# Turning rows over for cross attention: from TensorE transposes to grouped loads and 32x32 blocks on VectorE

## The chip, the cores and the metric

The kernel runs on one core of a Trainium2 chip. The metric is the device time of one execution in microseconds (us). The core has a matrix engine (TensorE, PE in the rows, with its weight loads as PEld), a vector engine (VectorE, DVE), a scalar engine (ScalarE, ACT), GpSimd (POOL) and SyncE (SP), whose queue issues most of the DMA transfers. Each engine takes its own instructions in the order in which they were listed when the program was built, and waits on semaphores where it needs another engine's result.

## The reference, cut to what matters

One encoder layer: a token mixer, then cross attention of 1024 rows into 256 memory tokens, then a mixture of experts. All is f32. The change concerns the cross attention alone:

```
def memory_cross_attention(h, hm, w_q, w_kv, w_o):
    q = (h @ w_q).reshape(Bq, S, N_XATTN_HEADS, XATTN_HEAD_DIM)
    kv = (hm @ w_kv).reshape(Bq, M, 2, N_XATTN_HEADS, XATTN_HEAD_DIM)
    k, v = kv[:, :, 0], kv[:, :, 1]
    s = jnp.einsum('bshd,bmhd->bhsm', q, k).astype(jnp.float32) * (XATTN_HEAD_DIM ** -0.5)
    p = jax.nn.softmax(s, axis=-1).astype(h.dtype)
    o = jnp.einsum('bhsm,bmhd->bshd', p, v).reshape(Bq, S, N_XATTN_HEADS * XATTN_HEAD_DIM)
    return o @ w_o
...
x = x + memory_cross_attention(rms_norm(x, g_xattn[l]), rms_norm(mem, g_mem[l]),
                               w_q_x[l], w_kv_x[l], w_o_x[l])
```

## The kernel before

The 1024 rows are eight tiles of 128, taken in the order of `corder`. The query weights and the keys are multiplied together ahead (the matrix `aH` + `aL`, 1024 x 1024), and so are values and output weights (`vH` + `vL`). So a tile x (128 x 1024) needs two products: its **scores**, x times `a` (4 heads x 256 memory tokens, so 1024 columns), and after the softmax its **values**, p times `v`, 1024 columns that are added to x.

A matmul contracts over the partitions, so both products need their left operand turned over: 1024 columns as eight blocks of 128 partitions. `transposed` (L732) does that: eight PE transposes against the identity (L738) into two PSUM tiles of 128 x 512, `tp`. Every f32 operand is then cut in two by `split` (L107): the high part is a cast on ACT (L108, `xH<-tp`), the low part a subtraction on DVE (L109, `xL<-tp,xH`). `mm3` makes three matmuls of one product: high times high (L100), high `x` in the low matrix (L101), low `x` in the high matrix (L102; only this one reads `xL`).

The loop over the tiles of the scores has two halves of 512 columns (two heads each), 24 matmuls each. Behind the first half's matmuls it calls `prep` for the next tile (L746): load the row tile from `x1_dram`, transpose and split it, sum its squares. Then each half's softmax on DVE and ACT: row maximum (L862), its scaling (L863), two exponentials (ACT, L866), reciprocal (L868), two scalings (L871). The probabilities go to `p_dram` (L872). Of the first tile `prep` is called before the loop, ahead of the last `proj` (the mixer's output product, `pc` in the rows), into the PSUM tile `pa`.

The loop over the tiles of the values has two halves of 24 matmuls as well. Behind the first half's it calls `attend_T` for the next tile (L835): load the probabilities again, transpose and split them. The result is added to x on DVE (L1111), its squares are summed on ACT (L1120), GpSimd makes the reciprocal root (L1122, L1123), and DVE writes the normed row `hn` (L1128). Between them DVE does the routing of the tiles before to the experts, in many small operations.

Which instruction comes when on each engine is not written out here: a scheduler lists the instructions of each engine when the program is built. SP's queue carries the loads of the tiles, the stores of the probabilities and the loads of expert weights (`wraw`), in one order.

Of the kernel before, what the change touches and what calls it, by code (L numbers as in the profile page):

```python
# [9 lines left out]
F32 = mybir.dt.float32  # L10
F32R = mybir.dt.float32r
BF16 = mybir.dt.bfloat16
I32 = mybir.dt.int32
AF = mybir.ActivationFunctionType
ALU = mybir.AluOpType
# [3 lines left out]
P = 128  # L19
D = 1024  # L20
S = 1024
KT = D // P
NT = S // P
NH = 4
DH = 128
NMEM = 256
# [22 lines left out]
def tile_hybrid_encoder(ctx: ExitStack, tc: tile.TileContext,  # L49
                        x, mem, pcols, rows, w_tm, w_cm, w_sT, w_out,  # L50
                        w_kv, w_qT, w_o, w_r, g_moe, g_final, w_gu, w_dn, out, dbg=None):
    nc = tc.nc

    def tpool(**kw):
        return tc.tile_pool(reuse_waits="tile", **kw)
# [33 lines left out]
    p_dram = tc.dram_tile([NT, P, NH * NMEM], F32, name="p_dram")  # L89
# [3 lines left out]
    x1_dram = tc.dram_tile([NT, P, D], F32, name="x1_dram")  # L93

    def rstd_of(dst, ss, n, eps, width=1):
        nc.gpsimd.tensor_scalar(dst, ss, 1.0 / n, eps, op0=ALU.mult, op1=ALU.add)  # L96
        nc.gpsimd.tensor_tensor(dst, dst, mhalf[:, 0:width], op=ALU.pow)  # L97

    def mm3(o, ah, al, bh, bl, first, last):
        nc.tensor.matmul(o, ah, bh, start=first, stop=False)  # L100
        nc.tensor.matmul(o, ah, bl, start=False, stop=False)  # L101
        nc.tensor.matmul(o, al, bh, start=False, stop=last)  # L102

    def f32(t):
        return t.bitcast(F32)

    def split(h, l, r):  # L107
        nc.scalar.copy(h, r)  # L108
        nc.vector.tensor_tensor(l, r, f32(h), op=ALU.subtract)  # L109
# [138 lines left out]
    with ExitStack() as pa:  # L248
# [24 lines left out]
        with tc.manual_schedule(engines={mybir.EngineType.DVE, mybir.EngineType.Activation}):  # L273
# [3 lines left out]
            for kp in range(4):  # L277
                tp = ptr.tile([P, 2, NMEM], F32, name="tp")
# [105 lines left out]
    with tpool(name="work1b", bufs=2, side="right") as work, \  # L384
# [6 lines left out]
        for g in range(4):  # L391
            cm_unit(g + 2)
            for hf in range(2):
                ps = cm_half(g, hf)
                sp = ptr.tile([P, 4, P], F32, name="tp")
                for j in range(4):
# [12 lines left out]
                                               op0=ALU.add, op1=ALU.mult)  # L409
# [5 lines left out]
    with tpool(name="work2", bufs=2, side="right") as work:  # L415
# [9 lines left out]
        for c in range(12):  # L425
# [16 lines left out]
            if c < 8:  # L442
                for hf in range(2):
# [3 lines left out]
                                            op0=ALU.mult, op1=ALU.add)  # L447
                    for w in range(1, 5):
                        nc.vector.scalar_tensor_tensor(cv, pre[:, a + w:a + w + 512], cw[:, c, w:w + 1], cv,
                                                       op0=ALU.mult, op1=ALU.add)  # L450
# [23 lines left out]
    work = pS2.enter_context(tpool(name="work3", bufs=2, side="right"))  # L474
# [252 lines left out]
    pp = pM.enter_context(tpool(name="pp", bufs=2, side="right"))  # L727
    pA = ExitStack()
    apool = pA.enter_context(tpool(name="apool", bufs=1, side="right"))
# [3 lines left out]
    def transposed(src, tile, hl=None):  # L733
        hl = hl or (pp.tile([P, KT, P], F32R, name="xH"), pp.tile([P, KT, P], F32R, name="xL"))
        for g in range(2):
            tp = tile()
            for j in range(4):
                nc.tensor.transpose(tp[:, j], src[:, (g * 4 + j) * P:(g * 4 + j + 1) * P], ident)  # L738
            gs = slice(g * 4, g * 4 + 4)
            split(hl[0][:, gs], hl[1][:, gs], tp)  # L740
        return hl

    def sums(junk, xt, ss):
        nc.scalar.activation(junk, xt, AF.Square, accum_out=ss)

    def prep(c, tile):  # L746
        xt = pp.tile([P, D], F32, name="x1t")
        nc.sync.dma_start(xt, x1_dram[c])
        ss = pp.tile([P, 2], F32, name="ss")
        hl = transposed(xt, tile)  # L750
        sums(xt, xt, ss[:, 0:1])
        rstd_of(ss[:, 0:1], ss[:, 0:1], D, RMS_EPS)
        nc.gpsimd.tensor_scalar(ss[:, 1:2], ss[:, 0:1], -1.0, None, op0=ALU.mult)
        return ss, hl

    for kt in range(KT):
# [3 lines left out]
        aL.append(pair[:, sl])  # L760
        evac(aH[kt], aL[kt], araw[kt // 2][:, sl], gx[:, kt:kt + 1])
    nxt = prep(corder[0], lambda: psa.tile([P, NH, P], F32, name="pa"))
    proj(corder[-1])
    pY.close()
# [18 lines left out]
    work = pV.enter_context(tpool(name="work5", bufs=2))  # L783
# [50 lines left out]

    def attend_T(c):  # L835
        prf = work.tile([P, NH * NMEM], F32, name="pr")
        nc.sync.dma_start(prf, p_dram[c])
        return transposed(prf, trt)

    def attend_x(c):  # L840
        xt = pp.tile([P, D], F32, name="x1t")
        nc.sync.dma_start(xt, x1_dram[c])
        return xt

    for t, c in enumerate(corder):
        ss, (xH, xL) = nxt
        pr = work.tile([P, NH, NMEM], F32, name="pr")
        mx = rw.tile([P, NH], F32, name="smx")
        sm = rw.tile([P, NH], F32, name="ssm")
        for hf in range(2):  # L850
            ps = pmm.tile([P, 512], F32, name="mm")
            sl = slice(hf * 512, hf * 512 + 512)
            for kt in range(KT):
                mm3(ps, xH[:, kt], xL[:, kt], aH[kt][:, sl], aL[kt][:, sl], kt == 0, kt == KT - 1)
            if hf == 0:
                if t + 1 < NT:
                    nxt = prep(corder[t + 1], trt)
                else:
                    nxt = attend_T(corder[0])
            psv = ps.rearrange("p (h m) -> p h m", h=2)  # L860
            hs = slice(hf * 2, hf * 2 + 2)
            nc.vector.tensor_reduce(mx[:, hs], psv, axis=AX.X, op=ALU.max)  # L862
            nc.vector.tensor_scalar(mx[:, hs], mx[:, hs], ss[:, 1:2], None, op0=ALU.mult)  # L863
            for i in range(2):
                h = hf * 2 + i
                nc.scalar.activation(pr[:, h], psv[:, i], AF.Exp, bias=mx[:, h:h + 1], scale=ss[:, 0:1],  # L866
                                     accum_out=sm[:, h:h + 1])
            nc.vector.reciprocal(sm[:, hs], sm[:, hs])  # L868
            for i in range(2):
                h = hf * 2 + i  # L870
                nc.vector.tensor_scalar(pr[:, h], pr[:, h], sm[:, h:h + 1], None, op0=ALU.mult)  # L871
        nc.sync.dma_start(p_dram[c], pr.rearrange("p h m -> p (h m)"))  # L872
        r = work.tile([P, D], F32, name="hn")
        nc.sync.dma_start(r, vw_dram[t])
        split(vH[t], vL[t], r)
# [37 lines left out]
    src = {b: (w_gu[b], w_dn[b]) for b in range(FIXED)}  # L913
# [167 lines left out]
    xt = attend_x(corder[0])  # L1081
    prep_r(2)
    prev = None
    for t, c in enumerate(corder):
# [9 lines left out]
        for hf in range(2):  # L1094
            ps = pmm.tile([P, 512], F32, name="mm")
            sl = slice(hf * 512, hf * 512 + 512)
            for i in range(8):
                mm3(ps, pH[:, i], pL[:, i], vH[i][:, sl], vL[i][:, sl], i == 0, i == 7)
                if t and hf == 0 and i == 1:
                    route_x(prev, 1)  # L1100
                if t > 1 and hf == 0 and i == 2:
                    route_s(t - 2, corder[t - 2])
                if t and hf == 0 and i == 4:
                    route_l(prev)
                if hf and i == 4:
                    route_x(c, 0)
            if t and hf:
                route_w(prev)
                route_p(t - 1, prev)
                route_r(prev)  # L1110
            nc.vector.tensor_tensor(xt[:, sl], xt[:, sl], ps, op=ALU.add)  # L1111
            if hf == 0:
                hn = work.tile([P, D], F32, name="hn")
                if not last:
                    nxt = attend_T(nx)
                else:
                    xgs.append(pp.tile([P, D], F32, name="x1t"))
                    nc.gpsimd.memset(xgs[0], 0.0)
                prep_r(min(3 + 2 * t, NRA))
            nc.scalar.activation(hn[:, sl], xt[:, sl], AF.Square, scale=D ** -0.5, accum_out=ssq[:, hf:hf + 1])  # L1120
# [12 lines left out]
        else:  # L1133
            prev = c
            xt = xn
# [449 lines left out]
```

## Time and profile before

| | |
|---|---|
| median of 3 runs | 1384.59 us (1383.39 to 1385.33) |
| the profiled execution | 1385.45 us, span 1383.7 us |
| mean granted clock of TensorE | 0.971 |
| busy: PE, DVE, ACT, POOL | 1271.4, 793.1, 612.9, 188.3 us |

The span is the time from the first to the last instruction; the profiled execution's own time has 1.75 us around it. Busy times are sums over all stages, so the stage of the change has to be read by itself. In the rows, a matmul's start shows when PE took it up; matmuls overlap, so the steps from start to start tell what one costs, not the durations. "[idle before <-releaser]" is the time for which the engine stood still before the instruction and what ended it. The granted clock (PEclk) is a share of full speed: 1.00 is 2.4 GHz and 0.50 is 1.2 GHz.

### The profile page before, as it was taken

The numbers are of one execution on the slowest core, as the hardware profiler recorded it, in microseconds if no ns is written. First come the engines' busy times: TensorE is split into PE (matmuls) and PEld (weight loads), VectorE is DVE, ScalarE is ACT, GpSimd is POOL, SyncE is SP. The second block draws the span as 40 slices with busy tenths as digits, with TensorE's granted clock in tenths as the row PEclk, the third lists the DMA queues.
The fourth block names the chain that finished last, engine by engine and source line by source line (L and its number), as shares of the span: only waits on it lengthen the run. The fifth ranks groups of instructions, "written<-read, shape, count | busy, mean of one in ns | idle before, by whom it ended". The sixth has DMA issues, their size and how long they took to land. (4 is left out here: it accounts for less than half of the span.)

```text
span 1383.7 us, 18356 instructions
## 1 busy us (share of the span) xinstructions
PE 1271.4 (92%) x6505; PEld 970.5 (70%) x6505; DVE 793.1 (57%) x1532; ACT 612.9 (44%) x1043; POOL 188.3 (14%) x283
## 2 busy tenths in 40 slices
PE   6899999999897899999999679999999999999980
PEld 6899888888886788888888557655555555566530
DVE  5643465883477765753467668645546454667512
ACT  7632343331474442653222248545446454556522
POOL 2000100000021111110133221112111111100012
PEclk9999999999999999999999879999999999999995
DMA  8820122311798652543963568999999999999967
GB/s 317 267 74 1 36 80 84 92 38 42 236 310 283 215 187 100 199 141 108 338 248 112 213 223 313 388 399 402 399 393 395 392 377 391 378 386 379 384 230 265
DMA packets 86750, 339.53 MB, mean 245 GB/s; under 512 B 12008, under 2 KB 24488, under 8 KB 62081
## 3 DMA queue, kind: packets, MB, share of 16 engines
q1 hardware_dynamic: 72672, 304.53, 59.0%
q0 software_dynamic: 11536, 26.31, 6.6%
q10 hardware_dynamic: 2448, 7.51, 1.4%
q8 instruction: 52, 0.85, 0.3%
q14 instruction: 42, 0.34, 0.1%
HBM read 297.06 MB, written 50.67 MB: 251 GB/s over the span
## 5 line engine op out<-in xcount | busy, mean ns | idle before, releaser
L109 DVE TENSOR_TENSOR wl<-wraw,wh 128x1024 fp32r<-128x1024 f32 (+2 forms) x276 | 325.2, 1210 | 118.2 <-ACT wh L108 106.5
L108 ACT CAST wh<-wraw 128x1024 fp32r<-128x1024 f32 (+2 forms) x276 | 277.7, 1037 | 97.4 <-PE mm L101 29.8
L1191 PE MATMUL gu<-wraw,xTn 128*64 128x512 f32 x512 | 118.2, 598 | 0.5 <-DMA wraw<-in_w_gu_dram 0.5
L101 PE MATMUL gu<-wl,xH 128*128 128x512 f32 x272 | 109.4, 402 | 1.3 <-DVE wl L109 1.1
L102 PE MATMUL gu<-wh,xL 128*128 128x512 f32 x272 | 107.6, 396 | 0.0
L100 PE MATMUL gu<-wh,xH 128*128 128x512 f32 x272 | 99.3, 405 | 2.4 <-ACT wh L108 1.7
L100 PE MATMUL mm<-hH,wh 128*128 128x512 f32 x256 | 100.3, 392 | 0.8 <-ACT wh L108 0.8
L101 PE MATMUL mm<-hL,wh 128*128 128x512 f32 x256 | 100.2, 391 | 0.0
L102 PE MATMUL mm<-hH,wl 128*128 128x512 f32 x256 | 100.0, 391 | 0.0
L1191 PEld LDWEIGHTS gu<-wraw,xTn 128*64 128x64 f32 x512 | 34.2, 136 | 63.8 <-issue 59.7
L108 ACT CAST xH<-tp 128x512 fp32r<-128x512 f32 x64 | 35.4, 589 | 67.7 <-PE tp L738 67.4
L101 PEld LDWEIGHTS gu<-wl,xH 128*128 128x128 f32 x272 | 52.2, 192 | 16.9 <-DVE wl L109 5.7
L100 PEld LDWEIGHTS gu<-wh,xH 128*128 128x128 f32 x272 | 51.9, 191 | 17.2 <-ACT wh L108 4.4
L101 PE MATMUL mm<-wl,hH 128*128 128x384 f32 (+2 forms) x192 | 61.7, 321 | 0.0
L102 PE MATMUL mm<-wh,hL 128*128 128x384 f32 (+2 forms) x192 | 61.6, 321 | 0.0
L100 PE MATMUL mm<-wh,hH 128*128 128x384 f32 (+2 forms) x192 | 61.3, 319 | 0.0
L1228 PE MATMUL y<-wraw,mTn 128*64 128x512 f32 x256 | 60.2, 602 | 1.1 <-ACT mTn L1216 1.1
L101 PE MATMUL y<-wl,mH 128*128 128x512 f32 x136 | 56.3, 414 | 5.2 <-DVE wl L109 5.2
L102 PEld LDWEIGHTS gu<-wh,xL 128*128 128x128 f32 x272 | 51.9, 191 | 11.4 <-DVE xL L109 0.2
L109 DVE TENSOR_TENSOR xL<-tp,xH 128x512 fp32r<-128x512 f32 x64 | 42.7, 685 | 23.7 <-ACT xH L108 23.5
L100 PEld LDWEIGHTS mm<-hH,wh 128*128 128x128 f32 x256 | 48.1, 188 | 10.7 <-ACT wh L108 1.1
L102 PEld LDWEIGHTS mm<-hH,wl 128*128 128x128 f32 x256 | 48.1, 188 | 10.2 <-issue 0.2
(418 smaller groups left out, 2730.5 us busy)
## 6 DMA issues: line engine op xcount, KB each, us to landing
wraw<-in_w_gu_dram SPq DMA_DIRECT2D x128, 1024.0 KB, 22.5
wraw<-in_w_dn_dram SPq DMA_DIRECT2D x64, 1024.0 KB, 23.3
wraw<-in_w_kv_dram SPq DMA_DIRECT2D x16, 512.0 KB, 5.2
xt<-in_x_dram SPq DMA_DIRECT2D x16, 512.0 KB, 5.8
wraw<-in_w_cm_dram SPq DMA_DIRECT2D x16, 512.0 KB, 3.7
x1t<-x_dram SPq DMA_DIRECT2D x16, 512.0 KB, 3.9
wraw<-in_w_tm_dram SPq DMA_DIRECT2D x8, 520.0 KB, 5.3
wraw<-in_w_qT_dram SPq DMA_DIRECT2D x8, 512.0 KB, 7.1
```

What stands on the lines that cost most here:

```text
L100: nc.tensor.matmul(o, ah, bh, start=first, stop=False)
L101: nc.tensor.matmul(o, ah, bl, start=False, stop=False)
L102: nc.tensor.matmul(o, al, bh, start=False, stop=last)
L108: nc.scalar.copy(h, r)
L109: nc.vector.tensor_tensor(l, r, f32(h), op=ALU.subtract)
L1191: nc.tensor.matmul(ps[q * 64:q * 64 + 64].rearrange("p (b c) -> p b c", b=2), xT[:, kt, hf * 64:hf * 64 + 64], r4[:, k, :, q * 256:q * 256 ...
L1228: nc.tensor.matmul(ps[q * 64:q * 64 + 64], mT[:, k, i * 64:i * 64 + 64], r[:, k * 1024 + q * 512:k * 1024 + q * 512 + 512], start=i == 0 a ...
```

## The change

The PE transposes of both stages go. In the scores, `prep` loads the row tile a second time, into a new tile `xb` (two buffers), by 16 DMAs of 32 partitions each, in pieces of 32 elements (128 B): partition group c receives the columns k*128 + c*32 + j of all rows, so that a row block t of 32 rows and a column group stand together. What is left to turn over are 32 x 32 blocks, for which DVE has a transpose: `turned_over` does two of 128 x 512 for a tile, into the same PSUM tiles, and the splits follow as before. The plain load `x1t` stays, for the sum of squares. In the values, the exponentials and the scalings write the probabilities in the order (c h k j), so that the loads from `p_dram` can put them in groups by four DMAs with pieces of 1 KB.

```
+    def turned_over(src, tile):
+        hl = pp.tile([P, KT, P], F32R, name="xH"), pp.tile([P, KT, P], F32R, name="xL")
+        sv = src.rearrange("p (t k j) -> p t k j", t=4, j=32)
+        for g in range(2):
+            tp = tile()
+            gs = slice(g * 4, g * 4 + 4)
+            nc.vector.transpose(tp.rearrange("p k (t i) -> p t k i", t=4), sv[:, :, gs])
+            split(hl[0][:, gs], hl[1][:, gs], tp)
+        return hl
...
-        hl = transposed(xt, tile)
+        xb = apool.tile([P, D], F32, name="xb", bufs=2)
+        xbv = xb.rearrange("p (t k j) -> p t k j", t=4, j=32)
+        xs = x1_dram[c].rearrange("(t i) (k c j) -> c i t k j", t=4, c=4, j=32)
+        for q in range(4):
+            for t in range(4):
+                nc.sync.dma_start(xbv[q * 32:q * 32 + 32, t], xs[q, :, t])
+        hl = turned_over(xb, tile)
...
-        nc.sync.dma_start(prf, p_dram[c])
-        return transposed(prf, trt)
+        for q in range(4):
+            nc.sync.dma_start(prf[q * 32:q * 32 + 32].rearrange("p (t f) -> p t f", t=4),
+                              p_dram[c].rearrange("(t i) (c f) -> c i t f", t=4, c=4)[q])
+        return turned_over(prf, trt)
...
-        pr = work.tile([P, NH, NMEM], F32, name="pr")
+        pr = work.tile([P, NH * NMEM], F32, name="pr")
+        prv = pr.rearrange("p (c h k j) -> p h k c j", c=4, h=NH, k=2)
...
-                nc.scalar.activation(pr[:, h], psv[:, i], AF.Exp, bias=mx[:, h:h + 1], scale=ss[:, 0:1],
+                nc.scalar.activation(prv[:, h], psv[:, i].rearrange("p (k c j) -> p k c j", k=2, c=4), AF.Exp, bias=mx[:, h:h + 1], scale=ss[:, 0:1],
...
-                nc.vector.tensor_scalar(pr[:, h], pr[:, h], sm[:, h:h + 1], None, op0=ALU.mult)
-        nc.sync.dma_start(p_dram[c], pr.rearrange("p h m -> p (h m)"))
+                nc.vector.tensor_scalar(prv[:, h], prv[:, h], sm[:, h:h + 1], None, op0=ALU.mult)
+        nc.sync.dma_start(p_dram[c], pr)
```

The change adds lines, so a line of the kernel after has another number: the row maximum is L883 there, the scaling of the probabilities L892, the residual add L1132, `hn` L1149, and DVE's transpose L751.

The listing of DVE's instructions for a boundary of two tiles in the middle of the scores, before: both halves of a tile, with the split of the next tile's transposes behind the maximum of the first half.

```order
L862 TENSOR_REDUCE smx<-mm 128x2
L863 TENSOR_SCALAR smx<-smx,ss 128x2
L109 TENSOR_TENSOR xL<-tp,xH 128x512 x2
L868 RECIPROCAL ssm<-ssm 128x2
L871 TENSOR_SCALAR pr<-pr,ssm 128x256 x2
L862 TENSOR_REDUCE smx<-mm 128x2
L863 TENSOR_SCALAR smx<-smx,ss 128x2
L868 RECIPROCAL ssm<-ssm 128x2
L871 TENSOR_SCALAR pr<-pr,ssm 128x256 x2
```

The same engine at the same place after the change, both halves of a tile again.

```order
L883 TENSOR_REDUCE smx<-mm 128x2
L884 TENSOR_SCALAR smx<-smx,ss 128x2
L889 RECIPROCAL ssm<-ssm 128x2
L892 TENSOR_SCALAR pr<-pr,ssm 128x2x4x32 x2
L883 TENSOR_REDUCE smx<-mm 128x2
L884 TENSOR_SCALAR smx<-smx,ss 128x2
L889 RECIPROCAL ssm<-ssm 128x2
L892 TENSOR_SCALAR pr<-pr,ssm 128x2x4x32 x2
L751 STREAM_TRANSPOSE tp<-xb 128x4x4x32 x2
L109 TENSOR_TENSOR xL<-tp,xH 128x512 x2
```

The next tile's transposes and split have moved behind all of the second half's softmax. So it is at the boundaries into tiles 2, 4, 5, 6 and 7, counted from 0; into tile 3 they stand behind the second half's L884, and into tile 1 behind its L883.

The second place is the start of the scores on DVE, before: the splits of the first tile (from `pa`), then the low parts of the keys' matrix (L113), the last output tiles of the mixer (L704) and a constant (`kcol`).

```order
L109 TENSOR_TENSOR xL<-pa,xH 128x512
L109 TENSOR_TENSOR yl<-ogc,yh 128x512
L109 TENSOR_TENSOR xL<-pa,xH 128x512
L113 SCALAR_TENSOR_TENSOR wraw<-wraw,gx,aH_5184 128x1024
...
L113 SCALAR_TENSOR_TENSOR wraw<-wraw,gx,aH_5191 128x1024
L828 TENSOR_SCALAR kcol<-kcol 128x1
L862 TENSOR_REDUCE smx<-mm 128x2
```

After the change the same stretch of DVE ends in this way.

```order
L113 SCALAR_TENSOR_TENSOR wraw<-wraw,gx,aH_5191 128x1024
L846 TENSOR_SCALAR kcol<-kcol 128x1
L751 STREAM_TRANSPOSE pa<-xb 128x4x4x32 x2
L109 TENSOR_TENSOR xL<-pa,xH 128x512 x2
L883 TENSOR_REDUCE smx<-mm 128x2
```

The first tile's split has moved from ahead of the eight L113 to behind them.

The third place is DVE at the end of the first value tile, before: the adds of its two halves, with the split of the second tile between.

```order
L1111 TENSOR_TENSOR x1t<-x1t,mm 128x512
L109 TENSOR_TENSOR xL<-tp,xH 128x512 x2
L1111 TENSOR_TENSOR x1t<-x1t,mm 128x512
L1128 SCALAR_TENSOR_TENSOR hn<-x1t,rs_6223,gmb 128x1024
```

After the change:

```order
L1132 TENSOR_TENSOR x1t<-x1t,mm 128x512 x2
L1149 SCALAR_TENSOR_TENSOR hn<-x1t,rs_6305,gmb 128x1024
L751 STREAM_TRANSPOSE tp<-pr 128x4x4x32 x2
L109 TENSOR_TENSOR xL<-tp,xH 128x512 x2
```

The transposes and the split of the second value tile stand behind both adds and behind `hn`. On PE the matmuls keep their order. On SP the 16 loads of `xb` of the tile after next stand around the store of the probabilities, and the expert weights' loads, which began in the first score tile, begin in the last.

## Rows read from the trace of the kernel before

**Rows 1.** The page: span, busy time of PE, its granted clock in tenths by slice.

```profile
span 1383.7 us, 18356 instructions
...
PE 1271.4 (92%) x6505; PEld 970.5 (70%) x6505; DVE 793.1 (57%) x1532; ACT 612.9 (44%) x1043; POOL 188.3 (14%) x283
...
PEclk9999999999999999999999879999999999999995
```

**Rows 2.** Windows of the scores, the values and the expert stage.

```profile
core 0: us, PE busy (x) PEld busy (x) DVE busy (x) ACT busy (x) POOL busy (x), PEclk, DMA share, GB/s
...
565.00:661.00 96.00, 96.00 (x451) 78.97 (x450) 49.18 (x105) 41.81 (x99) 10.18 (x26) 1.00 0.46 161
661.00:785.00 124.00, 121.47 (x676) 101.79 (x675) 77.07 (x370) 35.63 (x90) 30.77 (x41) 1.00 0.61 224
785.00:1383.00 598.00, 521.50 (x2320) 319.41 (x2319) 323.73 (x410) 294.70 (x379) 93.69 (x81) 0.94 0.94 357
```

**Rows 3.** Timeline of PE in the scores: start, duration, engine, line, operation, tiles.

```profile
595.08 1.03 PE L738 MATMUL tp<-ident,x1t 128*128 128x128 f32 x8
...
596.42 0.40 PE L102 MATMUL mm<-aH,xL 128*128 128x512 f32 x1
...
606.83 0.39 PE L102 MATMUL mm<-aH,xL 128*128 128x512 f32 x1
607.06 1.03 PE L738 MATMUL tp<-ident,x1t 128*128 128x128 f32 x8
...
613.49 0.39 PE L100 MATMUL mm<-aH,xH 128*128 128x512 f32 x1
```

**Rows 4.** Timeline of DVE there, with the idle time before each.

```profile
608.32 1.29 DVE L109 TENSOR_TENSOR xL<-tp,xH 128x512 fp32r<-128x512 f32 x2
...
613.69 0.69 DVE L862 TENSOR_REDUCE smx<-mm 128x2 f32<-128x512 f32 x1 [1.93 <-PE mm L102]
...
615.98 0.17 DVE L868 RECIPROCAL ssm<-ssm 128x2 f32<-128x2 f32 x1 [1.33 <-ACT pr L866]
616.18 0.62 DVE L871 TENSOR_SCALAR pr<-pr,ssm 128x256 f32<-128x256 f32 x2
```

**Rows 5.** Timeline of ACT there.

```profile
607.70 1.07 ACT L108 CAST xH<-tp 128x512 fp32r<-128x512 f32 x2 [3.64 <-PE tp L738]
```

**Rows 6.** Timeline of DVE at the start of the scores.

```profile
566.94 2.48 DVE L113 SCALAR_TENSOR_TENSOR wraw<-wraw,gx,aH 128x1024 fp32r<-128x1024 f32 x2
569.33 0.15 DVE L828 TENSOR_SCALAR kcol<-kcol 128x1 f32<-128x1 f32 x1
```

**Rows 7.** Timeline of PE there: the first matmul of the scores.

```profile
565.68 0.40 PE L100 MATMUL mm<-aH,xH 128*128 128x512 f32 x1
```

**Rows 8.** Timeline of DVE in the values.

```profile
673.90 0.69 DVE L1111 TENSOR_TENSOR x1t<-x1t,mm 128x512 f32<-128x512 f32 x1 [4.43 <-PE mm L102]
676.63 1.28 DVE L1128 SCALAR_TENSOR_TENSOR hn<-x1t,rs,gmb 128x1024 f32<-128x1024 f32 x1 [2.04 <-POOL rs L1123]
```

**Rows 9.** Timeline of PE in the mixer, behind an idle stretch.

```profile
370.25 0.39 PE L100 MATMUL pc<-wh 128*128 128x256 f32 x1 [2.07 <-ACT wraw L505]
```

**Rows 10.** Windows of 1 us there, PE alone: length, busy, clock, DMA share, GB/s.

```profile
371.00:372.00 1.00, 1.00 (x9) 0.88 0.86 340
372.00:373.00 1.00, 1.00 (x7) 0.50 0.98 328
...
375.00:376.00 1.00, 1.00 (x9) 0.92 0.77 225
```

**Rows 11.** The same behind another idle stretch.

```profile
438.00:439.00 1.00, 0.08 (x1) 1.00 0.94 305
...
440.00:441.00 1.00, 1.00 (x4) 0.51 1.01 412
...
443.00:444.00 1.00, 1.00 (x8) 0.78 0.83 336
```

**Rows 12.** DMA from 262 to 266 us, where 512-B pieces are stored.

```profile
q1 hardware_dynamic: 528, 0.26, 21.3%
```

**Rows 13.** Instructions of line L748, the load of a row tile: minimum, median, maximum ns.

```profile
L748 SPq DMA_DIRECT2D x1t<-x_dram x8: 319/320/424, 543.2 to 621.8; - x8
```

## The prediction, made before the changed kernel ran

> **What bounds the kernel now.** I read the page first: TensorE (PE) is busy 1271.4 of 1383.7 us, at a granted clock of nine tenths or more in nearly every slice [rows 1]. That is an average over stages, so the windows come next. In the scores (565 to 661 us) PE is busy all 96 us at clock 1.00, and VectorE (DVE) 49.18 us, ScalarE (ACT) 41.81 us. In the values (661 to 785) PE is busy 121.47 of 124 us. In the expert stage behind them the DMA share is 0.94 [rows 2]. The prefetch before that stage is bounded by its buffers, and the listing of SP's queue shows as many weight loads ahead of the stage in both kernels. So a microsecond that PE gains or loses in the scores and the values moves the end by about a microsecond (an estimate; the trace can't show it).
>
> Then the timeline of PE in one score tile. The eight transposes begin at 595.08 and next at 607.06, a period of 11.98 us. Between them stand 48 matmuls, of which the third begins at 596.42 and the last at 606.83, 45 steps of 0.2313 us [rows 3]. 48 steps are 11.10 us, so a set of eight transposes costs **0.88 us** of PE.
>
> **What is removed.** Sixteen sets (eight score tiles, eight value tiles): 16 x 0.88 = **14.1 us** of PE. Both stages are bound by PE, so I count it whole.
>
> **What is added on VectorE.** Each set becomes two transposes of 128x512 f32 into PSUM (L751). The trace before has none. The nearest rows are the subtraction `xL<-tp,xH`, 1.29 us for two from PSUM at the same width, and the row maximum over 512 columns, 0.69 [rows 4]. I take 0.69 for one and 0.60 to the next one's start. Bounds: half of that (0.35), if it reads faster from SBUF; double (1.3), if the turned access costs twice. As busy time this is 16 x 1.3 = 21 us on an engine that is half idle: nothing, if it stood beside PE's work. Whether it does is a matter of order.
>
> The Trainium skill ("VectorE: DVE Perf Modes", section "The three transpose paths") gives 311 ns for one 128x128 block on VectorE, in bf16 and into SBUF, and says that only 32x32 blocks are turned. An estimate by that figure is 8 x 0.311 = 2.5 us for a set, where I take 1.3 from the rows; the thirteen waits below would be 1.2 us longer each, and the time some 16 us more. No run so far shows which.
>
> **Where the order puts them.** DVE takes its work strictly in the listed order. Before, a tile's `xL` stood behind the *first* half of the tile ahead, 24 matmuls (5.5 us) before it was wanted. After, in the quoted piece, the transposes stand behind reduce, scaled maximum, reciprocal and both scalings of the *second* half. That reduce reads PE's last matmul of the tile. So PE has nothing to do until DVE has gone through the softmax and then through transposes and splits; the next tile's matmuls need `xH`, the third one `xL`.
>
> Call E the time at which PE issues the next tile's first matmul when nothing holds it, 613.49 in the tile shown [rows 3]. The reduce begins at 613.69 (E+0.20), the reciprocal, held by ACT's exponentials, at 615.98, and the two scalings run from 616.18 to 616.80 (E+3.3) [rows 4]. Then the first transpose to E+3.95, the second to E+4.55; ACT's cast `xH` (1.07 for two, so some 0.6 for the first) [rows 5] beside the second, to E+4.6; `xL` to E+5.3. The third matmul, due at E+0.46, starts at E+5.3: **4.85 us** lost. Five of the seven tile boundaries in the scores have this order (into tiles 2, 4, 5, 6 and 7, counted from 0). Into tile 3 the transposes stand behind reduce and scaled maximum only: by the same steps, with ACT busy on exponentials, 3.3. Into tile 1 they stand right behind the reduce: 2.5. The set for the first value tile stands behind a first half: nothing.
>
> **The start.** The first set had its `xL` at 555 us. Now it stands behind the last subtraction for the keys and `kcol`. The last two of those end at 569.42, `kcol` begins at 569.33 [rows 6]; without the two `xL` ahead of them they end 1.2 us earlier at most, and since they also wait for ACT I take 0.95. First transpose 568.4, `xL` finished 570.35. PE's first score matmul began at 565.68 [rows 7], now 0.88 earlier, 564.8, and its third at 565.26: **5.1 us** lost. Scores in all: 5.1 + 2.5 + 3.3 + 5 x 4.85 = 35.2.
>
> **The values.** Into the second tile the transposes stand behind both residual adds and `hn`. From an add's start to the start of `hn` the trace has 2.73 us (673.90 to 676.63), with ACT and GpSimd between, and `hn` takes 1.28 [rows 8]. So: add at E+0.2, `hn` ends E+4.2, two transposes and splits to `xL` at E+6.2, the third matmul due at E+0.46: 5.7. The other boundaries by the same steps from what the listing has ahead: behind the last add alone 2.6 (into tile 3, counted from 0), behind the add and up to eight small routing operations 3.3 and 3.1 (into tiles 4 and 6), with `hn` ahead of `xL` 4.65 (into tile 5), nothing into tiles 2 and 7. Sum **19.4**.
>
> Waits 35.2 + 19.4 = 54.6, less the 14.1: **+40.5 us**.
>
> **The clock.** Every one of those 13 waits leaves PE idle for 2.5 us or more. Where PE last stood for 2.07 us, until 370.25 [rows 9], the granted clock fell to its lower level (0.50, 1.2 GHz) over 371.9 to 375.1 while matmuls ran, and came back [rows 10]: (1-0.88) + 3 x 0.50 + 0.08 = 1.70 us lost. After a stretch that ends with PE busy 0.08 us in 438 to 439 it was 0.51 to 0.78 in four windows from 440, 1.71 lost with the two between at 0.50 [rows 11]. I charge 1.70 to each of 13: **+22 us**; the bounds are nothing and that.
>
> **The DMAs.** Each score tile loads its row a second time, 16 transfers on SP, 4,096 pieces of 128 B, 256 for each of 16 engines. One issue costs SP 0.32 us [rows 13], so 5.1 us for sixteen, in a tile of 12 to 17 us, and nothing on SP but stores and loads waits behind. No row before has 128-B pieces. The nearest is a store of 512-B pieces: 528 packets took 21.3% of 16 engines' 4 us [rows 12], 25.8 ns each. Bounds: a quarter of that by bytes (6.5 ns) and, since a smaller piece may cost more than a larger one, up to four times (103 ns). I take 25.8: 6.6 us a tile, with about 4.4 us for the three other 512 KB transfers of the tile, hidden in the 16 us between one set's release and the next set's use. At 45 ns a piece (11.6 us + 4.4) it stops being hidden. The store of the probabilities and the four loads of 1 KB pieces move as many bytes as before: nothing.
>
> On this the Trainium skill ("DMA: Bandwidth & Descriptors", sections "Specifications" and "Rules for kernel authors") speaks against the change: below 512 B a transfer is done by read-modify-write, and many small transfers should be made one. If that doubled the 25.8 ns, the estimate is 13.2 + 4.4 = 17.6 us a tile, just what a tile takes with its wait, and the time some 1447 to 1455. No row so far shows it.
>
> **Sum** for the profiled run: 1385.45 + 40.5 + 22 = 1448; the median of the runs shown is 0.9 lower, so **1447 us**.
>
> **Rivals.** *Waits without the lower clock*, 1425: 13 idle stretches of 2.5 to 6 us end in tiles of 11 us of unbroken work, and the clock might stay up; against it stand both rows cited, after shorter and like stretches. *Late pieces*, 1450 to 1540: DMA instead of DVE sets the tile from 45 ns a piece. At 60 ns a tile is 15.4 + 4.4 = 19.8 us, against 11.1 + 4.85 + 1.7 = 17.6 with its wait and clock; seven tiles x 2.2 = +15, 1462. At 103 ns it is 30.8 us, +13 x 7, near 1540. For it stands only that no row so small exists; against it the 25.8. *The other side*, 1370: the transposes are ready in time, PE's 14.1 us stay gained. It decides at a mean wait of 14.1 / 13 = 1.1 us, clock left out; since the reduce alone begins 0.2 behind PE's last matmul and two transposes and a split follow even in the best of the thirteen (2.5), the listing would have to be no guide to the chip. *It does nothing*: only if waits and gain cancel, the same 1.1 us.
>
> **How the numbers follow.** Waits with the clock lost 0.62, waits alone 0.15, late pieces 0.17, the other side 0.04, no change 0.02. The likeliest case's own range is 1432 (half the clock's falls, and 4 less for cheap transposes, 13 x 0.35) to 1463 (transposes at double: 13 x 1.2 = 16 more). With waits alone below, less 4 for cheap transposes, and the nearer part of the late pieces above, the range is 1422 to 1475. About 0.2% is what a measurement of this kernel can tell from no change: faster by more 0.04, within 0.02, slower 0.94.
>
> **What would show it.** In the profile after: PE's idle time in the scores should be near 35 us, in gaps of 4.5 to 5.5 us put down to ACT `xH` or DVE `xL`, with granted clock windows of 0.50 behind each; L751 at 0.6 to 0.7 us; the period between the first matmuls of two tiles 16 to 18 us. If the first transpose of a tile waits for a DMA and not for its turn behind the scalings, the late pieces are right. The prediction is wrong if DVE's transposes start before PE's last matmul of the tile ends, if no clock falls, or if the expert stage takes the delay up in its own slack.

## The result: 4.1% slower

The changed kernel takes 1439.62 us (median of 4 runs, 1438.63 to 1446.61) against 1384.66 beside it: a ratio of **1.0409** (95% interval 1.0375 to 1.0442), 55.0 us more. 1447 was forecast, with a range of 1422 to 1475.

The page of the profile after, where it answers to [rows 1]: PE has gained 9 us of busy time although 128 transposes are gone, and its mean granted clock is 0.956 in place of 0.971; the queue that carries SP's loads has 110,944 packets in place of 72,672.

```profile
span 1437.8 us, 18317 instructions
...
PE 1280.6 (89%) x6377; PEld 971.2 (68%) x6377; DVE 813.1 (57%) x1564; ACT 616.0 (43%) x1043; POOL 189.5 (13%) x283
...
q1 hardware_dynamic: 110944, 308.73, 59.4%
```

The windows of the scores, the values and the expert stage after, which answer to [rows 2]: PE is busy 95.69 us of 127.5 in the scores and its mean clock there is 0.91; in the values 121.06 of 138.5, at 0.94. The first value matmul starts at 695.28 us (before: 661.36), 33.9 later; the first gate matmul of the routed experts (L1212, at 936.0) is 53.6 us later and the end 54.1. So the delay arises in these two stages and the expert stage gives none of it back.

```profile
564.00:691.50 127.50, 95.69 (x369) 75.05 (x369) 56.96 (x117) 39.88 (x92) 7.38 (x23) 0.91 0.49 130
691.50:830.00 138.50, 121.06 (x601) 99.41 (x600) 86.26 (x373) 34.27 (x86) 25.75 (x38) 0.94 0.60 196
830.00:1437.00 607.00, 529.90 (x2357) 326.18 (x2355) 327.93 (x428) 300.05 (x391) 102.33 (x84) 0.94 0.94 356
```

What PE waited for between 540 and 850 us (total us, times, longest): thirteen waits for the high part `xH` of a tile, 45.2 us. Before, PE waited for nothing in the scores: it was busy for all of their 96 us [rows 2].

```profile
PE mm L100 <- ACT xH L108: 45.2, 13, 5.4
```

The timeline of PE, the first six of them, with the idle time in front of each: start of the scores, then the boundaries into tiles 1 to 5.

```profile
568.73 0.79 PE L100 MATMUL mm<-aH,xH 128*128 128x512 f32 x1 [4.72 <-ACT xH L108]
584.01 0.51 PE L100 MATMUL mm<-aH,xH 128*128 128x512 f32 x1 [2.04 <-ACT xH L108]
599.76 0.50 PE L100 MATMUL mm<-aH,xH 128*128 128x512 f32 x1 [4.45 <-ACT xH L108]
615.62 0.50 PE L100 MATMUL mm<-aH,xH 128*128 128x512 f32 x1 [2.82 <-ACT xH L108]
631.39 0.79 PE L100 MATMUL mm<-aH,xH 128*128 128x512 f32 x1 [4.45 <-ACT xH L108]
648.51 0.79 PE L100 MATMUL mm<-aH,xH 128*128 128x512 f32 x1 [4.45 <-ACT xH L108]
```

The timeline of DVE at the boundary into tile 2. PE's last matmul of tile 1 ends just before 595.35. The reduce waits for it (1.94), the reciprocal for ACT, and only behind the scalings come the transposes. They wait for nothing but their turn: no idle time stands in front of them.

```profile
595.35 0.69 DVE L883 TENSOR_REDUCE smx<-mm 128x2 f32<-128x512 f32 x1 [1.94 <-PE mm L102]
596.08 0.23 DVE L884 TENSOR_SCALAR smx<-smx,ss 128x2 f32<-128x2 f32 x1
597.64 0.17 DVE L889 RECIPROCAL ssm<-ssm 128x2 f32<-128x2 f32 x1 [1.33 <-ACT pr L887]
597.84 0.61 DVE L892 TENSOR_SCALAR pr<-pr,ssm 128x256 f32<-128x256 f32 x2
598.37 1.31 DVE L751 STREAM_TRANSPOSE tp<-xb 128x512 f32<-128x512 f32 x2
599.74 1.29 DVE L109 TENSOR_TENSOR xL<-tp,xH 128x512 fp32r<-128x512 f32 x2
```

Windows of 1 us of PE behind that gap: here the granted clock is 1.00 while PE stands, and falls some 0.6 us after it has started again at 599.76 (0.67 is the mean of the window from 600). Behind the other four gaps of 4.45 us it is low from PE's first matmul on, which takes 0.79 us there in place of 0.50 (631.39 and 648.51 above).

```profile
599.00:600.00 1.00, 0.23 (x1) 1.00 0.73 287
600.00:601.00 1.00, 1.00 (x3) 0.67 0.91 273
601.00:602.00 1.00, 1.00 (x4) 0.50 0.33 52
...
603.00:604.00 1.00, 1.00 (x4) 0.63 0.39 60
604.00:605.00 1.00, 1.00 (x6) 1.00 0.28 44
```

The two lines that the change adds, each with its least, median and greatest time in ns: DVE's transposes of `xb` take 702 ns, SP's issue of one 128-B-piece load 607 ns, against 320 for the load of a whole row tile [rows 13].

```profile
L751 DVE STREAM_TRANSPOSE tp<-xb x14: 682/702/726, 582.6 to 682.0; 128x512 f32<-128x512 f32 x14
L767 SPq DMA_DIRECT2D xb<-x_dram x128: 539/607/1387, 553.8 to 675.2; - x128
```

### The profile page after: what moved, and what is told of

The parts are those of the page before. It is cut to its first block, busy times and chain, and to the rows that moved or that the text cites. A ratio compares the mean times of both kernels' runs of the same rounds, so it can differ in the third digit from the quotient of the medians.

```text
span 1437.8 us, 18317 instructions
## 1 busy us (share of the span) xinstructions
PE 1280.6 (89%) x6377; PEld 971.2 (68%) x6377; DVE 813.1 (57%) x1564; ACT 616.0 (43%) x1043; POOL 189.5 (13%) x283
## 3 DMA queue, kind: packets, MB, share of 16 engines
q1 hardware_dynamic: 110944, 308.73, 59.4%
## 5 line engine op out<-in xcount | busy, mean ns | idle before, releaser
L1212 PE MATMUL gu<-wraw,xTn 128*64 128x512 f32 x512 | 118.4, 598 | 0.9 <-DMA wraw<-in_w_gu_dram 0.8
L100 PE MATMUL mm<-aH,xH 128*128 128x512 f32 x128 | 55.0, 430 | 31.8 <-ACT xH L108 31.8
L1212 PEld LDWEIGHTS gu<-wraw,xTn 128*64 128x64 f32 x512 | 34.2, 136 | 64.6 <-issue 60.2
L100 PE MATMUL mm<-vH,xH 128*128 128x512 f32 x128 | 54.7, 427 | 13.4 <-ACT xH L108 13.4
```

The source lines that it names most:

```text
L1212: nc.tensor.matmul(ps[q * 64:q * 64 + 64].rearrange("p (b c) -> p b c", b=2), xT[:, kt, hf * 64:hf * 64 + 64], r4[:, k, :, q * 256:q * 256 ...
```

## The experiments

Theory A, from the prediction: the place of the transposes in DVE's listing makes the waits. Rival B: the sixteen small loads make them, being late. Rival C: two transposes and the splits are simply too much for DVE. Each run is told against the kernel before, measured beside it. The ratio is the recorded one; it is not exactly the quotient of the two medians.

**One stage at a time.** e1 gives the values their PE transposes back (with the plain load and the plain order of the probabilities, not shown in the cut), e2 the scores (without the loads of `xb`).

```
# e1, in attend_T and the softmax                # e2, in prep
-  return turned_over(prf, trt)                  -  hl = turned_over(xb, tile)
+  return transposed(prf, trt)                   +  hl = transposed(xt, tile)
```

e1: 

> The scores as in the change, the values with PE's transposes again. Order theory (the listing puts the transposes behind the second half's softmax): the eight waits of the scores stay (31.8 us) with their clock falls; the values start 33.9 us late as in the profile after, and nothing is added there: about 1384.7 + 34 = 1419. Rival, the delay is spread by something the two stages share (DMA traffic, the lower clock carried on): the values would stay slower, 1430 or more.

Measured: 1420.49 against 1384.3, 1.0252 (1.0208 to 1.0296), +36. PE's waits for `xH` are 31.8 us in 8, as in the change. The scores carry 36 of the 55.

e2: 

> The scores with PE's transposes, the values as in the change. Order theory: five waits in the values, 13.4 us, less 7 us of transposes, plus clock: about 1384.7 + 20 = 1404. With e1 it should add up to the whole (+55). Rival, the waits in the values come from the scores' delay (weight loads pushed into the values): no waits here and 1378.

Measured: 1389.75 against 1384.3, 1.0037 (1.0016 to 1.0057), +5.4. Not 1404: with the scores as before the scheduler lists the values in another way, and three waits are left of five, 8.1 us. I had priced this kernel by the listing of another. The two runs sum to 41.6, not 55; that the rest belongs to how the stages are listed together is argued, not shown.

**The order alone.** e3 lists the second half's maximum, and in the values the second half's add, behind the next tile's splits.

```
+ with tc.issue_after(last_xL) if hf else ExitStack():
      nc.vector.tensor_reduce(mx[:, hs], psv, axis=AX.X, op=ALU.max)
...
+ with tc.issue_after(last_xL) if hf and not last else ExitStack():
      nc.vector.tensor_tensor(xt[:, sl], xt[:, sl], ps, op=ALU.add)
```

e3: 

> The change, with one edit: the second half's maximum (scores) and the second half's add (values) are listed behind the next tile's transposes and splits. Order theory: twelve of thirteen waits go, the first tile's 4.7 us and its clock fall stay: 1384.7 - 14.1 + 6.5 = 1377. Rival, the loads: a load of the grouped pieces took SP 0.68 us in the profile after, not the 0.32 I charged, so 16 of them and the tile's three other transfers are 12.1 us, over the 11.1 us of matmuls: PE would wait about 1 us a tile for them, 1384; if the loads land later than that, DVE now stalls in front of them and the time stays over 1400.

Measured: 1422.8 against 1384.3, 1.0265 (1.0224 to 1.0305). Rival B shows itself here: what DVE waited for in the scores, and one of these waits in its timeline:

```profile
DVE tp L753 <- DMA xb<-x_dram: 18.9, 7, 4.3
```

```profile
628.06 1.32 DVE L753 STREAM_TRANSPOSE tp<-xb 128x512 f32<-128x512 f32 x2 [4.28 <-DMA xb<-x_dram]
```

So the late place had hidden a second lateness: with the transposes moved forward, the loads are not there. Theory A alone is not enough. Why they are late stands in SP's timeline:

```profile
620.11 0.33 SPq L897 DMA_DIRECT2D p_dram<-pr  x1
620.48 5.88 SPq L769 DMA_DIRECT2D xb<-x_dram  x9
```

The loads land soon after their issue (median 2.3 us), and SP is not always at work: between 585 and 675 us it stood 16.0 us in front of six stores of probabilities, which wait for DVE's scalings of a second half. Nine of a tile's sixteen loads are listed behind such a store, and the transposes at 628.06 wait for the last of these nine. The rows read as a loop: transposes (628.06), the second half's softmax, the next store (634.77), nine loads of 0.65 us each (to 641.02), the next transposes (643.44). The expectation above had counted SP's time alone (12.1 us a tile) and not this place in its queue.

**The order with cheap loads.** The mixer stores each row tile a second time, in grouped order, and four loads of 1 KB pieces (432 ns each) take the place of sixteen. e5 forces the late listing at every boundary, e6 the early one (in the values ahead of the routing too, and for the first tile ahead of most of the L113), e11 forces nothing.

```
+ xg = ywork.tile([P, D], F32, name="xg", bufs=1)
+ nc.gpsimd.tensor_copy(xg.rearrange("p (c k j) -> p k c j", c=4, j=32),
+                       xt.rearrange("p (k c j) -> p k c j", c=4, j=32))
+ nc.sync.dma_start(x1g_dram[c], xg)
...
- for q in range(4):
-     for t in range(4):
-         nc.sync.dma_start(xbv[q * 32:q * 32 + 32, t], xs[q, :, t])
+ for q in range(4):
+     nc.sync.dma_start(xb[q * 32:q * 32 + 32].rearrange("p (t f) -> p t f", t=4),
+                       x1g_dram[c].rearrange("(t i) (c f) -> c i t f", t=4, c=4)[q])
# e5 alone, behind the scalings of the second half
+ with tc.issue_after(last_scaling):
+     nxt = nxt[0], turned_over(*nxt[1])
```

e5: 

> The change with cheap loads: the mixer also stores each row tile in grouped order (GpSimd copies it, one more store a tile), so that four loads of 1 KB pieces replace the sixteen of 128 B; the next tile's transposes are put behind the second half's scalings at every boundary. Order theory: PE waits at all seven boundaries of the scores, 4.5 us each, and at the first tile, 36 us, with clock falls; with values about as in the change near 1440. Loads theory (the wait is for the loads, whatever the order): no waits in the scores, near 1395.

Measured: 1440.26 against 1385.17, 1.0408 (1.0376 to 1.044), the change's own time. PE's waits between 555 and 800 us:

```profile
PE mm L101 <- ACT xH L109: 43.6, 11, 5.5
```

With loads that are there in time the late listing costs as much as the change does: the listing is enough for such a loss by itself (DVE never waits for `xb` in this trace). That the two times are equal is in part chance: e5 is later than the change into tiles 1 and 3 (waits of 4.80 and 5.45 us in place of 2.04 and 2.82), so that its scores take 137.0 us, to the first value matmul, in place of 126.6, and its values wait less.

e6: 

> The same cheap loads, with the transposes and splits of the next tile listed ahead of the second half's maximum (scores) and of the second half's routing and add (values), and the first tile's ahead of the keys' subtractions. If lateness in the listing and slow loads are both needed for the loss and both are mended: PE's 14.1 us are gained, 1384.7 - 14 = 1371, faster than before. Rival, in the values the loads of the probabilities land late behind the expert weights whatever the order (one gap of 2.6 us with its clock fall in the run before): 1375 to 1380. Rival, VectorE too full: 1385 or more.

Measured: 1382.99 against 1385.17, 1.0000 (0.9982 to 1.0018): the loss is gone, but not the 14 us gained. The scores are mended: from their first matmul (568.21) to the first value matmul (658.6) they take 90.4 us in place of 95.7, with one wait of 2.1 us in front of them and one clock fall behind it. Two waits in the values remain, 3.2 and 1.5 us, and there DVE waits for the probabilities.

e11: 

> The change with the cheap loads of the scores alone, nothing forced in the listing. The scheduler, which takes the loads to be there sooner, lists the transposes of most score tiles behind a first half by itself; into the last score tile and in the values they still stand behind a second half. If the listing and not the loads makes the waits: in the scores a wait at the first tile (4.7 us) and into tile 7 (2 to 5 us) only, the values as late as in the change (+18): 1384.7 - 7 + 9 + 4 clock + 11 + 5 clock, about 1405. Rival, cheap loads alone mend it: 1385 or less.

Measured: 1392.99 against 1386.86, 1.0043 (1.0028 to 1.0057), where 1405 was expected. From the first matmul at 571.24 to the first value matmul at 662.05 the scores take 90.8 us: no boundary waits, into tile 7 neither, only the start (5.4 us). This run differs from the change by its loads (and the mixer's copy and store) alone: the loads are what leads the scheduler to the late listing; make them cheap, and the listing of the scores mends itself. In the values, whose loads are the same as in the change, PE still waits 5.4, 2.0 and 0.8 us for `xH`, each time behind a late listing.

**Whose time the loads take.** e8 is e3 with half of the sixteen loads on GpSimd's queue.

```
-  nc.sync.dma_start(xbv[q * 32:q * 32 + 32, t], xs[q, :, t])
+  (nc.sync if t < 2 else nc.gpsimd).dma_start(xbv[q * 32:q * 32 + 32, t], xs[q, :, t])
```

e8: 

> The early listing of the earlier run (1422.8), with half of the sixteen 128-B loads issued by GpSimd. If SP's issue time (0.64 us each, 14 us a tile with the rest) is what makes the loads late: VectorE's waits for them (18.9 us) mostly go and the time falls to about 1390. Rival, the pieces themselves are slow on the DMA engines: waits as before, 1420.

Measured: 1387.35, 1.0016 (1.0000 to 1.0033), 35 us under e3, and of DVE's waits for `xb` one of 0.3 us is left. The pieces are as small as before, so it is not their size that made them late. What did is not told apart further: the issuing is shared, but SP's listing has changed with it as well. In e8 SP issues its eight loads of a tile from 609.63 to 614.89, all of them well ahead of the next transposes (619.73). A run that moved the store alone was not made. The DMA engines were not the limit: over 7 us of such loads in the change, 2854 packets took 32.4% of 16 engines, 36.3 engine-us, 12.7 ns each.

```profile
DMA packets 2854, 0.36 MB, mean 52 GB/s; under 512 B 2850, under 2 KB 2850, under 8 KB 2854
...
q1 hardware_dynamic: 2854, 0.36, 32.4%
```

**The clock.** e7 is the change with matmuls that nothing reads in seven of the gaps in the scores.

```
+ if hf == 0 and t:
+     for i in range(8 if t in (1, 3) else 18):
+         nc.tensor.matmul(ps, aL[0][:, 0:P], aH[0][:, 0:512], start=True, stop=True)
```

e7: 

> The change, with matmuls that nothing reads put on PE into seven of the eight gaps of the scores (18 of 128x512, 4.2 us, in the gaps of 4.45 us; 8 in the two shorter ones). The waits stay, only PE is kept at work in them. If the lower clock behind the gaps costs 1.7 us each as I charged: no granted clock under 1.00 from 590 to 695 us, and 1439.6 - 5 x 1.7 = 1431. Rival, the lower clock costs nothing since the matmuls behind it wait for other things anyway: 1439 to 1441.

Measured: 1434.53 against 1385.17, 1.038 (1.0353 to 1.0407): 49.4 us over the kernel before in place of the change's 55.0. The change's five falls between 590 and 695 us are gone; one has come where the change had none (618 to 622, behind a gap of which 2.61 us stayed open). The 5.6 us between the two are within the intervals (each some 4 to 5 us to either side), but the traces show the price directly, in the time from one tile's first matmul to the next one's. From tile 4 on, with a fall in each tile, it is 17.12, 17.19 and 17.05 us in the change; without one it is 15.77, 15.77 and 15.75 here. So a fall costs 1.3 to 1.4 us, where 1.70 was charged. The timeline of PE at the boundaries into tiles 2, 4 and 5, where the wait was 4.45:

```profile
601.24 0.50 PE L100 MATMUL mm<-aH,xH 128*128 128x512 f32 x1 [0.33 <-ACT xH L108]
634.35 0.50 PE L100 MATMUL mm<-aH,xH 128*128 128x512 f32 x1 [0.33 <-ACT xH L108]
650.12 0.50 PE L100 MATMUL mm<-aH,xH 128*128 128x512 f32 x1 [0.33 <-ACT xH L108]
```

**The values.** e4 has the scores as before and the values with e3's early listing; e10 lists the routing behind the splits as well and issues the loads of the probabilities from ACT's queue.

```
# e10, in attend_T
-  nc.sync.dma_start(prf[q * 32:q * 32 + 32]...
+  nc.scalar.dma_start(prf[q * 32:q * 32 + 32]...
# e10, in the loop over the value tiles
+  with tc.issue_after(last_xL):
       route_w(prev); route_p(t - 1, prev); route_r(prev)
```

e4: 

> The scores with PE's transposes, the values as in the change with the second half's add listed behind the next tile's transposes. Order theory: eight sets of PE transposes are saved and nothing waits: 1384.7 - 7.0 = 1377.7, faster than before. Rival, VectorE is too full in the values (10 of 15 us busy) for two more transposes wherever they stand: 1384 or more.

Measured: 1390.14 against 1384.3, 1.0042 (1.0024 to 1.006). A miss: the first transposes of the values stood 5.92 us for their data. The four loads had been listed between expert weights of 1 MB. Two more waits (2.0 and 1.6 us) stand behind routing operations that wait for PE.

```profile
673.18 1.32 DVE L753 STREAM_TRANSPOSE tp<-pr 128x512 f32<-128x512 f32 x2 [5.92 <-DMA pr<-p_dram]
```

e10: 

> The scores with PE's transposes, the values as in the change with the early listing ahead of the routing, and the loads of the probabilities on ScalarE's queue. Theory: eight sets, 7 us: 1377.5. Rival: 1384 as before, if the weights' traffic holds these loads up on any queue.

Measured: 1386.2 against 1386.86, 0.9999 (0.9985 to 1.0013). One wait is left, but it is 7 us long, at the second value tile, and the clock falls in it. The rival's 1384 is nearer than the theory's 1377.5: DVE stood 8.4 us there for the probabilities.

**Everything mended.** e9 is e6 with the first tile of the scores through PE and the probabilities' loads on ACT's queue.

```
-  hl = turned_over(xb, tile)
+  hl = turned_over(xb, tile) if c != corder[0] else transposed(xt, tile)
```

e9: 

> The run with cheap loads and the early listing (1383.0), with its two remaining waits mended: the first tile of the scores goes through PE's transposes as before (it waited 2.1 us and lost 1.7 us of clock), and the loads of the probabilities are issued by ScalarE's queue, past the expert weights (3.2 and 1.5 us). Order-and-loads theory: 15 of 16 sets saved, 13.2 us, nothing waits: 1372. Rival, the loads still land late since the weights fill the DMA engines themselves: 1378 to 1383.

Measured: 1379.28 against 1386.86, **0.9947** (0.9931 to 0.9963): faster than before, by half of what was expected, and within what the rival said (1378 to 1383). The scores take 88.75 us, eight times 48 matmuls without a gap, 6.9 less than the 95.7 before, as eight sets of 0.88 should give; the later value tiles follow each other at 14.3 us, where [rows 8]' stage had 15.2. What is lost again stands at the second value tile: PE's timeline, and DVE's waits for the probabilities.

```profile
673.63 0.80 PE L101 MATMUL mm<-vH,xH 128*128 128x512 f32 x1 [5.42 <-ACT xH L111]
```

```profile
DVE tp L758 <- DMA pr<-p_dram: 9.1, 2, 8.8
```

Between 655 and 675 us the transfers of SP's queue alone took 89.3% of the 16 DMA engines, and the five loads of probabilities that ACT issued landed 10.4 us (median) after their issue. That fits the rival, by which the weights fill the DMA engines themselves.

e12 puts those loads back on SP and lists the expert weights behind them (the first of the weights, ahead of the loop before, too).

```
+  with tc.issue_after(last_load_of_pr):
       prep_r(min(3 + 2 * t, NRA))
```

e12: 

> The mended kernel (1379.3 beside 1386.9), with the loads of the probabilities on SP again, and the expert weights' loads listed behind those of the next tile in place of ahead of them. In the run before, the second value tile's transposes waited 8.8 us for a load that was put behind three weight loads of 1 MB, and PE 5.4 us with 1.7 to 3.4 us of clock. Theory: that wait goes, the time is 13 us under before, about 0.990 of it. Rival, the weights that are put later come later to the expert stage and the gain is lost there: 0.995 as in the run before, or more.

Measured: 1383.19 against 1386.95, 0.9973 (0.9961 to 0.9985). A miss: the second tile's wait is gone, but another of 3.58 us came at the sixth, with its clock fall, and the other value tiles follow at 14.6 to 16.3 us, not at the 14.3 of e9's; why is open.

```profile
729.71 0.50 PE L101 MATMUL mm<-vH,xH 128*128 128x512 f32 x1 [3.58 <-ACT xH L111]
```

Loads on ACT's queue and weights behind the second tile's loads were not tried together.

## Why the prediction was right, point by point

**The listing.** All 13 waits came at the 13 boundaries named, none at the others, and the experiments with cheap loads show that this listing alone costs as much (e5), and that without it and with loads in time the loss is gone (e6). The mechanism was right; what made the scheduler list so late, the loads, the prediction did not see.

**The size of the waits** was 45.2 us against 54.6. In the scores: 4.72, 2.04, 2.82 and five of 4.45 against 5.1, 2.5, 3.3 and 4.85, so 31.8 against 35.2. Part of this is in the counting. The profile counts idle time from the end of the last matmul, 0.39 us after its start, and the prediction from where the next would have started, 0.23 us after it. Into tile 2:

```profile
594.93 0.39 PE L102 MATMUL mm<-aH,xL 128*128 128x512 f32 x1
600.49 0.29 PEld L102 LDWEIGHTS mm<-aH,xL 128*128 128x128 f32 x1 [0.43 <-DVE xL L109]
```

By the prediction's count the next matmul was due at 595.16; the first came at 599.76, 4.60 us late, and the third, which reads `xL`, at 600.49, 4.87 late. The prediction had 4.6 and 4.85. So at this boundary it is right to a few hundredths, with a wait for `xL` (0.43 us, of the weight load) behind the one for `xH`. Into tiles 1 and 3 PE has two more matmuls on `xH` ahead of the first that reads `xL`, and there it waits for `xH` alone. In the values 13.4 against 19.4, of which the largest miss is the boundary into tile 5: 0.67 against 4.65, with two waits of 1.83 and 1.40 us beside it that belong to routing and `xL`.

**The clock** was charged 1.70 us in 13 places. It fell in nine: not behind the gaps of 2.04, 2.82, 1.98 and 2.84 us, though it fell behind one of 2.51 (at 801) and had fallen behind one of 2.07 before [rows 9, 10]. At three it stayed down twice as long (3.4 us lost by the rows at the start, from 709 and from 781). By windows of 1 us it is 37.6 us of full-speed time lost between 540 and 910, against 15.4 in the same stages before, +22.2. So the term of 22 came out, but by another count, and that is luck: the nine falls are 20.5 of it, six of 1.70 and three of 3.42, where thirteen of 1.70 were forecast. Not all of it costs time, since some falls while PE stands (2.0 us lie in windows in which PE did not work at all), and by the tile times of e7 a fall of 1.70 costs 1.3 to 1.4.

**The sum.** -14.1 + 45.2 + 22.2 = +53.3, measured span +54.1. That these are so near is luck too: the clock is counted too high, and 3.4 us of other waits between 727 and 783 us are left out. The forecast, +62.5, lay 7.5 above the measured +55.0, by the waits that it had too long, above all in the values.

**VectorE's transposes**: 702 ns against 690 taken; by an estimate from the Trainium skill's figure ("VectorE: DVE Perf Modes", section "The three transpose paths") a set would have been 2.5 us. The trace has 1.31 for the two of a set, so the row of the same width was the better guide for this f32 form. Rival C falls: e9 runs the scores without a gap with these transposes in.

**The loads** are the term I had wrong, and it did no harm only because the late listing hid it. I took 25.8 ns for a piece and 0.32 us for an issue [rows 13]; a piece took 12.7 ns, and an issue 0.61, 0.65 from start to start. So sixteen are 10.5 us of SP and not 5.1. That "nothing on SP but stores and loads waits behind" left out what the loads themselves wait behind: in e3 a store in the middle of them. In the change no transpose of `xb` waited for a DMA; they came too late for that. So the place of the loads was hidden, as the prediction says, but not because there was slack to hide it in, as e3 shows. And I took the late listing as given: e11, with four loads in place of sixteen, has it no more in the scores, and its loss is 6.1 us in place of 55.0. What the Trainium skill says against small transfers ("DMA: Bandwidth & Descriptors", section "Rules for kernel authors"), that many should be made one, held in its conclusion. The doubling that the prediction estimated for read-modify-write does not show: at 12.7 ns a 128-B piece of these loads took half of what a 512-B piece of a store took [rows 12]. Loads in 512-B pieces were not run.

**The other rivals.** "Waits without the lower clock" (1425) is out by the windows. "Late pieces" (1450 and more) is out for the change, where no transpose of `xb` waited for a DMA. "The other side" (1370) is what the change would be worth by the prediction's count with both latenesses mended; the best version, e9, reached 7.6 of its 14 us.

## What to carry to other kernels

Moving work from the bounding engine to an idle one gains only if the idle engine does it before it starts to wait for the bounding one: read the place in the in-order listing first, then the busy time. When a scheduler puts an operation late, ask what it thinks it is waiting for; forcing the order without mending that wait moves most of the stall elsewhere (1440 to 1423), mending both gave 1383, no loss, and with two further changes (e9) 1379. Price a split load by the issuing queue, per transfer, before pricing its bytes, and see which of the transfers ahead of it in that queue has to wait for the compute that it feeds.

## What the runs showed of the hardware that was not expected

The issue of a load of 32 partitions in 128-B pieces takes SP 607 ns and GpSimd 584, of 32 partitions in 1 KB pieces 432, of 128 partitions of 4 KB 320 before the change and 374 in it (medians). The pieces themselves are cheap: 12.7 ns for 128 B in these loads, against 25.8 for 512 B in stores [rows 12]. And the clock's fall does not follow from a gap's length alone: the clock fell behind gaps of 2.07, 2.51 and (in e7) 2.61 us, and not behind others of 2.82 and 2.84.
